# A shorter first chunk of the contraction, and x transposed by a product with a diagonal matrix

## The chip, the core and the metric

One NeuronCore of one Trainium2 chip runs the kernel. Its engines work side by side, each on its own instructions in program order: PE (matrix products and transposes; PEld is its weight load), DVE and ACT (elementwise work), POOL, and SP, which here issues nearly all DMA. The metric is the device time of one execution in microseconds (us), lower is better.

## What is computed

A transformer block over 256 tokens of width 2048. The input is normalised per token, scaled and shifted by vectors that come from a second input c through the large matrix ada_w, and projected by w_in; two attention branches, an output projection and a feed-forward part follow.

```python
c_act = jax.nn.silu(c)
mod = c_act @ ada_w[l] + ada_b[l]
sh1, sc1, gt1, sh2, sc2, gt2 = jnp.split(mod, 6, axis=-1)
h = rms_norm(x, norm1_g[l]) * (1.0 + sc1[:, None]) + sh1[:, None]
proj = h @ w_in[l]
...
x = x + gt1[:, None] * ((g_gla * y_gla + g_moba * y_moba) @ w_out[l])
h = rms_norm(x, norm2_g[l]) * (1.0 + sc2[:, None]) + sh2[:, None]
a, u = jnp.split(h @ w_ffn_in[l], 2, axis=-1)
x = x + gt2[:, None] * ((jax.nn.silu(a) * u) @ w_ffn_out[l])
```

All weights are float32. Each product is made of three float32r products: a weight tile and an h tile are each split into a high part and the rest (low part), and high x high, high x low and low x high are summed.

## The kernel before

**Tiling.** The contraction of the input projection has 2048 rows of w_in, 16 K tiles of 128. Its columns are cut into twenty blocks of 512, of which 0 to 15 take part in the stages below: in blocks 2, 3 and 8 to 15 tokens stand on partitions (`prod_tok`, six products of 128x512 for one K tile), in 0, 1 and 4 to 7 columns do (`prod_T`, twelve of 128x256). One K tile of one block is called a unit below.

**Chunks and stages.** h needs G = norm1_g (1 + scale) and SH = shift, which are columns of silu(c) @ ada_w. They are computed in chunks of K tiles, CHUNKS. While stage i of `plan` runs products with the K tiles whose h is known, the next chunk of ada_w streams in and is summed up in the background. `plan` lists by stage the blocks and up to which K tile each goes: the first stage takes ten blocks to K tile 2, the second takes those ten and blocks 0 to 5 to K tile 4, then ten to 8, and six to 12. A block's partial sum is left in PSUM, and moved by ACT (L356) where it is the block's first, or added by DVE (L358, L360) to what it had.

**ada_w.** The first chunk is multiplied on PE (L155, `on_pe`), then summed over partitions by L180. The other chunks are summed on DVE: the first step is L163, the fifteen further ones L161, each over [128, 1024] (512 where the chunk has two K tiles). Behind the sixteenth, PE sums over partitions (L186), ACT copies the result (`rowsum`, L189), PE transposes it (L192), DVE makes G and SH (L199 to L201), and `make_h` makes h of the chunk's K tiles: its high part on ACT (L298), a copy (L299), its low part on DVE (L300). The background generator is advanced after each weight tile by `pace`.

**Weights.** `w_tiles`: SP issues a load of a raw tile (two K tiles by 512 columns; rawp, ten buffers, shared with x and ada_w), ACT makes the high part (L126), DVE the low part (L127), into five buffers each. Two blocks' accumulators are open at a time (four PSUM tiles).

**The head.** Four loads bring x. ACT squares it in eight pieces of 512 with sums (L264), DVE adds them up (L265), ACT takes the root (L258), DVE multiplies all of x by it in eight pieces (L269). `x_T` transposes two K tiles by four transposes on PE (L278) and copies them (L281), all eight of these pairs before the first product. Behind the first stage come late loads on SP (`wglr`, `gn`, four of `w2`), which the gated attention needs.

**What sets the order.** A scheduler lays the instructions of each engine out in a fixed row when the kernel is built, with offsets that pull some ahead: weight parts (HP), h (HPH), evictions (HPE). On the chip each engine goes through its row in order.

Of the kernel before, what the change touches and what calls it, by code (L numbers as in the profile page):

```python
# [8 lines left out]
F32 = mybir.dt.float32  # L9
# [16 lines left out]
CHUNKS = (2, 2, 4, 4, 4)  # L26
# [14 lines left out]
def block_kernel(ctx, tc, x, c, ada_w, ada_b, norm1_g, w_in, gate_w2, gate_b, gla_norm_g,  # L41
# [31 lines left out]
    xv = x.rearrange("(m p) (j n) -> m p j n", p=P, n=W)  # L73
    xs = [[None] * 4 for _ in range(2)]
    for j in (0, 2):
        for m in range(2):
            t = rawp.tile([P, 2, W], F32, name="x", tag="raw")
            nc.sync.dma_start(t, xv[m, :, j:j + 2, :])
            xs[m][j], xs[m][j + 1] = t[:, 0], t[:, 1]

# [23 lines left out]
    cs = const.tile([P, KT], F32, name="cs")  # L104
    act(cs, cT, AF.Silu)

# [9 lines left out]
    def w_tiles(w_ap, k0, k1, c0, ncols=W):  # L116
        """tiles of the contraction by ncols columns: (first K tile, [(hi, lo), ...])"""
# [22 lines left out]
    def gemv(src, width, acc, on_pe, start=False):  # L140
        """src: [p, k, 2, width] columns of ada_w. acc: sums over partitions to (what it held, with start) +
        silu(c) @ those columns; with on_pe, to the columns of group i over partitions 64*i..64*i+63 of its first half"""
# [28 lines left out]
    def ada_scale_shift(which, k0, n, on_pe):  # L171
        """G = norm_g * (1 + scale), SH = shift, for columns of tiles k0..k0+n, column on partition"""
# [5 lines left out]
        if on_pe:  # L178
# [3 lines left out]
        else:  # L182
            # the sum over partitions of quarter g to partitions 32g.., then columns of it to partitions
# [19 lines left out]
    def ada_gate(idx, dst):  # L203
        """dst[j] = columns j of the gate, the same on each partition"""
# [48 lines left out]
    ss = const.tile([P, 2, 4], F32, name="ss")  # L253
    rstd = const.tile([P, 2], F32, name="rstd")
    junk = const.tile([P, W], BF16, name="junk")

# [5 lines left out]
    for j in range(4):  # L262
        for m in range(2):
            act(junk, xs[m][j], AF.Square, accum_out=ss[:, m, j:j + 1])  # L264
    nc.vector.tensor_reduce(rstd, ss, AX.X, ALU.add)  # L265
    row_rstd(rstd, rstd, D)
    for j in range(4):
        for m in range(2):
            ts(xs[m][j], xs[m][j], rstd[:, m:m + 1], None, ALU.mult)  # L269
# [3 lines left out]
    def x_T(kp):  # L273
        ps = ax_ps()
        for i in range(2):
            k = 2 * kp + i
            for m in range(2):
                nc.tensor.transpose(ps[:, i * T + m * P:i * T + (m + 1) * P],  # L278
                                    xs[m][k // 4][:, (k % 4) * P:(k % 4 + 1) * P], ident)
        xnT[kp] = slot("xnT")  # L280
        (nc.vector.tensor_copy if kp % 2 else nc.scalar.copy)(xnT[kp], ps)  # L281

    first = ada_scale_shift(0, 0, kn, True)
    for i in range(8):
        if i == 7:
            w_first = w_tiles(w_in, 0, 2, GG)
            w_got = [next(w_first)]
        next(first)
        x_T(i)
# [13 lines left out]
    def prod_tok(ps, m, hi, lo, wt, k0, first, last):  # L303
        """ps[token, col] += sum over the given tiles of h^T w, for token tile m"""
# [8 lines left out]
    def prod_T(ps, i, hi, lo, wt, k0, first, last):  # L313
        """ps[col, (two col tiles, token)] += sum over the given tiles, for column tiles 2i, 2i+1; one group"""
# [27 lines left out]
    def in_block(bi, k0, k1):  # L342
        """adds tiles k0..k1 of the contraction to block bi"""
        kind, c0, scale, func = blocks[bi]
        ps = [mm_ps(), mm_ps()]
        for k, g in w_got or w_tiles(w_in, k0, k1, c0):
            for i in range(2):
                (prod_T if kind == "T" else prod_tok)(ps[i], i, hTh, hTl, g, k, k == k0, k + 2 == k1)
# [24 lines left out]
    def build_masks():  # L373
# [7 lines left out]
        # keep s xor t where t > s, else 999  # L381
# [7 lines left out]
        for i in (0, 2):  # L389
            # keep 0 where t - s >= 0  # L390
# [3 lines left out]
    def gla_gate(k):  # L394
        """adds tile k to the gate's low rank product, one of four partial sums"""
# [417 lines left out]
```

## Time and profile before

| | us |
|---|---|
| median of three runs | 1471.33 (1468.92 to 1472.06) |
| profiled execution, span | 1469.6 |
| PE busy | 1441.1 (98%) |
| DVE busy | 1034.8 (70%) |
| ACT busy | 694.7 (47%) |
| granted PE clock, mean | 0.997 |
| DMA over the span | 249 GB/s |

The span is from the first to the last instruction. A matmul's busy time overlaps the next one's, so spacing is read from the chain of waits, which gives start to start. By the trace the first product of the projection starts at 26.85 us, the second stage at 58.34, the third at 125.30; the four stages are over by about 255, and the rest of the span, over 1200 us, is the other parts.

### The profile page before, as it was taken

Reading aid. Unit: us, or ns where it says so; the run is one execution under the profiler, and the core shown is the slowest. Engines: PE = TensorE matmul, PEld = TensorE weight load, DVE = VectorE, ACT = ScalarE, POOL = GpSimd, SP = SyncE. Lnnn points to the kernel's source line nnn. Section 1 sums busy time; section 2 is a strip of 40 time slices with the busy share of each in tenths; the row PEclk is TensorE's granted clock in tenths of the full one; section 3 lists DMA queues with packets and bytes.
Section 4 is the critical chain, followed back from the end, with each engine's and each line's share of the span. In section 5 each row is a group of like instructions: output and inputs, shape, how many; then the busy total and the mean of one; then the engine's idle time right before and its main releaser. Section 6 shows DMA issues by size and latency. Waiting matters only on the chain.

```text
span 1469.6 us, 19460 instructions
## 1 busy us (share of the span) xinstructions
PE 1441.1 (98%) x7304; PEld 1202.0 (82%) x7304; DVE 1034.8 (70%) x1196; ACT 694.7 (47%) x921; POOL 11.1 (1%) x28
## 2 busy tenths in 40 slices
PE   6999999999999999999999999999999999999997
PEld 3787899998788878888888778888888888888887
DVE  4798988997799989797696677544555445554554
ACT  5645344635557544444654444444343444444443
POOL 1000000000000000000000000000000000000000
PEclk9999999999999999999999999999999999999999
DMA  9999999895546999999588888655666666666641
GB/s 332 328 315 344 340 317 328 255 358 174 180 151 202 367 332 336 332 312 362 176 304 267 271 264 296 188 184 187 196 192 196 190 188 189 192 189 209 198 153 58
DMA packets 191934, 365.61 MB, mean 249 GB/s; under 512 B 13880, under 2 KB 31516, under 8 KB 191840
## 3 DMA queue, kind: packets, MB, share of 16 engines
q1 hardware_dynamic: 189792, 361.15, 74.9%
q10 hardware_dynamic: 2048, 3.22, 0.7%
q8 instruction: 57, 0.93, 0.2%
q14 instruction: 37, 0.30, 0.1%
HBM read 362.23 MB, written 2.10 MB: 248 GB/s over the span
## 4 chain that ended last, share of the span: by engine, by line
PE 91%; DMA 5%; DVE 3%; issue 1%; ACT 1%; ACTq 0%; DVEq 0%
PE mm L311 25%; PE mm L309 25%; PE mm L310 25%; DMA araw<-in_ada_w_dram 4%; PE mm L325 3%; PE mm L323 3%; PE mm L324 3%; DVE wlo L127 1%; PE ax L619 1%; PE ax L444 1%; DVE acc L161 1%; DMA x<-in_x_dram 1%; PE ax L397 0%; ACT whi L126 0%; PE ax L278 0%
## 5 line engine op out<-in xcount | busy, mean ns | idle before, releaser
L127 DVE TENSOR_TENSOR wlo<-raw,whi 128x1024 fp32r<-128x1024 f32 x488 | 595.1, 1223 | 338.8 <-ACT whi L126 331.6
L126 ACT CAST whi<-raw 128x1024 fp32r<-128x1024 f32 x488 | 512.6, 1053 | 660.6 <-PE mm L311 478.7
L309 PE MATMUL mm<-whi,h2h 128*128 128x512 f32 x704 | 274.5, 390 | 1.3 <-ACT h2h L699 1.3
L310 PE MATMUL mm<-wlo,h2h 128*128 128x512 f32 x704 | 274.9, 391 | 0.1
L311 PE MATMUL mm<-whi,h2l 128*128 128x512 f32 x704 | 274.8, 391 | 0.0
L161 DVE SCALAR_TENSOR_TENSOR acc<-araw,cs,acc 128x1024 f32<-128x1024 f32 (+1 forms) x184 | 227.6, 1237 | 27.2 <-DMA araw<-in_ada_w_dram 26.1
L311 PE MATMUL mm<-whi,tl 128*128 128x512 f32 (+1 forms) x552 | 200.7, 364 | 0.0
L309 PE MATMUL mm<-whi,th 128*128 128x512 f32 (+1 forms) x552 | 200.4, 363 | 0.0
L310 PE MATMUL mm<-wlo,th 128*128 128x512 f32 (+1 forms) x552 | 200.2, 363 | 0.0
L309 PE MATMUL mm<-whi,hTh 128*128 128x512 f32 x448 | 176.7, 398 | 3.0 <-ACT hTh L298 3.0
L310 PE MATMUL mm<-wlo,hTh 128*128 128x512 f32 x448 | 176.4, 394 | 0.6 <-DVE wlo L127 0.6
L311 PE MATMUL mm<-whi,hTl 128*128 128x512 f32 x448 | 176.7, 395 | 0.0
L309 PEld LDWEIGHTS mm<-whi,h2h 128*128 128x128 f32 x704 | 132.2, 188 | 29.2 <-ACT h2h L699 2.2
L310 PEld LDWEIGHTS mm<-wlo,h2h 128*128 128x128 f32 x704 | 132.2, 188 | 27.8 <-DVE wlo L127 0.5
L311 PEld LDWEIGHTS mm<-whi,h2l 128*128 128x128 f32 x704 | 132.2, 188 | 26.9 <-DVE h2l L700 0.2
L310 PEld LDWEIGHTS mm<-wlo,th 128*128 128x128 f32 x552 | 104.2, 189 | 16.3 <-issue 0.4
L311 PEld LDWEIGHTS mm<-whi,tl 128*128 128x128 f32 x552 | 104.3, 189 | 15.9 <-issue 0.4
L309 PEld LDWEIGHTS mm<-whi,th 128*128 128x128 f32 x552 | 104.3, 189 | 15.6
L324 PE MATMUL mm<-hTl,whi 128*128 128x256 f32 x384 | 108.8, 284 | 0.0
L323 PE MATMUL mm<-hTh,whi 128*128 128x256 f32 x384 | 108.6, 284 | 0.0
L325 PE MATMUL mm<-hTh,wlo 128*128 128x256 f32 x384 | 108.1, 284 | 0.0
L309 PEld LDWEIGHTS mm<-whi,hTh 128*128 128x128 f32 x448 | 84.5, 189 | 21.5 <-ACT hTh L298 3.7
(201 smaller groups left out, 1283.0 us busy)
## 6 DMA issues: line engine op xcount, KB each, us to landing
araw<-in_ada_w_dram SPq DMA_DIRECT2D x176, 512.0 KB, 5.6
raw<-in_w_ffn_in_dram SPq DMA_DIRECT2D x176, 512.0 KB, 3.7
raw<-in_w_in_dram SPq DMA_DIRECT2D x160, 512.0 KB, 5.6
raw<-in_w_ffn_out_dram SPq DMA_DIRECT2D x88, 512.0 KB, 4.6
raw<-in_w_out_dram SPq DMA_DIRECT2D x32, 512.0 KB, 7.4
araw<-in_ada_w_dram SPq DMA_DIRECT2D x32, 256.0 KB, 6.0
raw<-in_w_up_moba_dram SPq DMA_DIRECT2D x16, 512.0 KB, 5.1
raw<-in_w_up_gla_dram SPq DMA_DIRECT2D x16, 512.0 KB, 7.8
```

Of the source, the lines that this page charges most:

```text
L126: nc.scalar.copy(hi, raw)
L127: tt(lo, raw, hi.bitcast(F32), ALU.subtract)
L161: stt(a, vq, cs[:, k:k + 1], a, ALU.mult, ALU.add)
L309: mm(ps, lhsT=xh, rhs=wh, start=f, stop=False)
L310: mm(ps, lhsT=xh, rhs=wl, start=False, stop=False)
L311: mm(ps, lhsT=xl, rhs=wh, start=False, stop=l)
L323: mm(o, lhsT=wh[:, sl], rhs=xh, start=f, stop=False)
L324: mm(o, lhsT=wh[:, sl], rhs=xl, start=False, stop=False)
L325: mm(o, lhsT=wl[:, sl], rhs=xh, start=False, stop=l)
L444: mm(ps[:, s], lhsT=e[:, s], rhs=e[:, s], start=True, stop=True)
L619: nc.tensor.transpose(ps[:, q * T + m * P:q * T + (m + 1) * P], src[m][:, (2 * i + q) * P:(2 * i + q + 1) * P], ident)
```

## The change

The chunks become 1, 1, 2, 4, 4, 4, and `plan` gets one stage more: ten blocks to K tile 1, blocks 0 to 5 to K tile 2, then the ten and the six to K tile 4 (three and two units of each), the last two as before. In a stage whose blocks take an odd number of K tiles the last weight tile is half as wide.

x is squared in four pieces of 1024, two on ACT and two on DVE; a dummy root ahead of them loads ACT's table early. x itself is left as it is: DVE multiplies the unit matrix by the norm factor of each token half (`diag`), and `x_T` multiplies x by that in full float32 products where it had transposes. Only the first pair of K tiles is done ahead of the first product; the other seven are written behind blocks 15, 10, 11, 6, 7, 8 and 9 of the first stage; in PE's row the scheduler has put seven of their 28 products between the sum over partitions of the first chunk and the first product, and 21 between the products of the first stage. A chunk of one K tile that is summed on DVE takes its partition sum as columns straight away.

```diff
-CHUNKS = (2, 2, 4, 4, 4)
+CHUNKS = (1, 1, 2, 4, 4, 4)
...
+    act(cs0, epst, AF.Sqrt)
...
-        if on_pe:
+        if n == 1 and not on_pe:
+            for i in range(2):
+                mm(ps[:, 2 * i:2 * i + 2], lhsT=acc[:, i * P:(i + 1) * P], rhs=ones[:, 0:2], start=True, stop=True)
+            pv = ps[:, 0:4].rearrange("p (e i a) -> p e a i", e=2, a=2)[:, :, 0:1]
+        elif on_pe:
...
-    for j in range(4):
-        for m in range(2):
-            act(junk, xs[m][j], AF.Square, accum_out=ss[:, m, j:j + 1])
+    for i, (m, j, t) in enumerate(xw):
+        sq = slots.tile([P, 2 * W], BF16, name="sq", tag="slot")
+        if i % 2:
+            nc.vector.tensor_tensor_reduce(sq, t, t, 1.0, 0.0, ALU.mult, ALU.add, ss[:, m, j:j + 1])
+        else:
+            act(sq, t, AF.Square, accum_out=ss[:, m, j:j + 1])
...
-    for j in range(4):
-        for m in range(2):
-            ts(xs[m][j], xs[m][j], rstd[:, m:m + 1], None, ALU.mult)
+    for m in range(2):
+        ts(diag[:, m], ident, rstd[:, m:m + 1], None, ALU.mult)
...
-                nc.tensor.transpose(ps[:, i * T + m * P:i * T + (m + 1) * P],
-                                    xs[m][k // 4][:, (k % 4) * P:(k % 4 + 1) * P], ident)
+                mm(ps[:, i * T + m * P:i * T + (m + 1) * P], lhsT=xs[m][k // 4][:, (k % 4) * P:(k % 4 + 1) * P],
+                   rhs=diag[:, m], start=True, stop=True)
...
-    for i in range(8):
-        if i == 7:
-            w_first = w_tiles(w_in, 0, 2, GG)
+    for i in range(4):
+        if i == 3:
+            w_first = w_tiles(w_in, 0, kn, GG)
             w_got = [next(w_first)]
         next(first)
-        x_T(i)
+    x_T(0)
...
-    plan = [[(b, 2) for b in (12, 13, 14, 15, 10, 11, 6, 7, 8, 9)],
+    plan = [[(b, 1) for b in (12, 13, 14, 15, 10, 11, 6, 7, 8, 9)],
+            [(b, 2) for b in range(6)],
...
+            if st == 0 and bi not in (12, 13, 14):
+                x_T(next(later_x))
```

Three places show how the rows of the engines move. The first is DVE at the end of the stage behind which h of K tiles 4 to 7 is made. In the kernel before, `acc_674` is the sum of the chunk, `acc_1340` that of the next chunk, `wlo` are low parts of weights:

```order
L161 SCALAR_TENSOR_TENSOR acc_674<-araw_1167,cs_108,acc_674 128x1024
L127 TENSOR_TENSOR wlo_1172<-raw_1170,whi_1171 128x1024
L161 SCALAR_TENSOR_TENSOR acc_674<-araw_1200,cs_108,acc_674 128x1024
L127 TENSOR_TENSOR wlo_1211<-raw_1209,whi_1210 128x1024
L127 TENSOR_TENSOR wlo_1254<-raw_1252,whi_1253 128x1024
L127 TENSOR_TENSOR wlo_1306<-raw_1304,whi_1305 128x1024
L127 TENSOR_TENSOR wlo_1324<-raw_1322,whi_1323 128x1024
L163 TENSOR_SCALAR acc_1340<-araw_1341,cs_108 128x1024
L199 TENSOR_TENSOR G0_124<-ax_1246,scb_114 128x4
```

In the changed kernel, at the same place, `acc_819` is the sum of the chunk and `acc_1459` that of the next; `r4` and `r5` are evictions of blocks 4 and 5 (L372 is L360 of before, L131 L127, L165 and L167 are L161 and L163, L207 is L199):

```order
L372 SCALAR_TENSOR_TENSOR r4_1_740<-mm_1325,r4_1_740 128x512
L131 TENSOR_TENSOR wlo_1469<-raw_1467,whi_1468 128x1024
L372 SCALAR_TENSOR_TENSOR r5_0_775<-mm_1371,r5_0_775 128x512
L372 SCALAR_TENSOR_TENSOR r5_1_776<-mm_1372,r5_1_776 128x512
L165 SCALAR_TENSOR_TENSOR acc_819<-araw_1235,cs_108,acc_819 128x1024
L131 TENSOR_TENSOR wlo_1490<-raw_1488,whi_1489 128x1024
L165 SCALAR_TENSOR_TENSOR acc_819<-araw_1272,cs_108,acc_819 128x1024
L131 TENSOR_TENSOR wlo_1515<-raw_1513,whi_1514 128x1024
L165 SCALAR_TENSOR_TENSOR acc_819<-araw_1319,cs_108,acc_819 128x1024
L167 TENSOR_SCALAR acc_1459<-araw_1460,cs_108 128x1024
L165 SCALAR_TENSOR_TENSOR acc_1459<-araw_1485,cs_108,acc_1459 128x1024
L165 SCALAR_TENSOR_TENSOR acc_1459<-araw_1506,cs_108,acc_1459 128x1024
```

The evictions of block 5, the last block of the stage, have come to DVE, and three steps of the chunk's sum now stand behind them; G follows behind the last row shown.

The second place is PE there. In the changed kernel (L337 is L325 of before, L194 and L200 are L186 and L192, L321 and L322 are L309 and L310), `mm_1372` is the second accumulator of block 5 and `hTh_222` holds h of K tiles 4 and 5:

```order
L336 MATMUL mm_1372<-hTl_229,whi_1374 128x256
L337 MATMUL mm_1372<-hTh_221,wlo_1375 128x256
L194 MATMUL ax_1356<-acc_819,ones_89 32x256 x4
L200 MATMUL ax_1363<-ident_84,rowsum_1361 128x128 x2
L321 MATMUL mm_1421<-whi_1424,hTh_222 128x512
L322 MATMUL mm_1421<-wlo_1425,hTh_222 128x512
```

In the kernel before, the sum over partitions stood some thirty products ahead of the end of block 5; it now stands behind the last one.

The third place is SP at the end of the first stage, in the changed kernel; `raw_536` is the first weight load of the second stage:

```order
L128 DMA raw_469<-in_w_in_dram 128x512
L128 DMA raw_500<-in_w_in_dram 128x512
L583 DMA wglr_104<-in_w_in_dram 128x16x16
L583 DMA gn_105<-in_gla_norm_g_dram 128x256
L583 DMA w2_103<-in_gla_gate_w2_dram 16x512 x4
L128 DMA raw_536<-in_w_in_dram 128x2x512
L153 DMA araw_567<-in_ada_w_dram 128x2x256 x2
```

The late loads stand behind the loads of the first stage and ahead of those of the second, as before, but behind ten tiles of half the size.

## Rows read from the trace of the kernel before

**Rows 1.** The page: busy time by engine, and the chain that ended last.

```profile
PE 1441.1 (98%) x7304; PEld 1202.0 (82%) x7304; DVE 1034.8 (70%) x1196; ACT 694.7 (47%) x921; POOL 11.1 (1%) x28
...
PE 91%; DMA 5%; DVE 3%; issue 1%; ACT 1%; ACTq 0%; DVEq 0%
```

**Rows 2.** Timeline of the head: start, duration, engine, line, operation.

```profile
13.55 1.28 ACT L258 ACT_TABLE_LOAD   x1 [0.27 <-DVE rstd L265]
...
15.38 3.26 DVE L269 TENSOR_SCALAR x<-x,rstd 128x512 f32<-128x512 f32 x8
...
23.55 1.06 PE L155 MATMUL ax<-araw,cpad 128*32 128x256 f32 x12
...
26.20 1.09 ACT L298 ACTIVATE hTh<-xnT,SH,G 128x256 fp32r<-128x256 f32 x2 [1.17 <-DVE G L200]
...
26.85 0.61 PE L309 MATMUL mm<-whi,hTh 128*128 128x512 f32 x1 [1.14 <-ACT hTh L298]
```

**Rows 3.** Busy time of each engine by window, granted clock, DMA share, GB/s.

```profile
0.00:10.00 10.00, 0.40 (x1) 0.18 (x1) 0.18 (x1) 5.59 (x11) 3.92 (x19) 1.00 0.80 254
10.00:20.00 10.00, 8.75 (x60) 3.98 (x61) 5.21 (x16) 5.91 (x14) 0.00 (x0) 1.00 1.08 353
...
26.80:31.00 4.20, 4.15 (x11) 3.19 (x12) 3.61 (x6) 2.93 (x5) 0.00 (x0) 0.59 1.07 370
...
58.00:67.00 9.00, 8.66 (x35) 6.12 (x36) 7.60 (x11) 5.75 (x8) 0.00 (x0) 1.00 1.05 390
67.00:100.00 33.00, 33.00 (x212) 29.84 (x211) 32.34 (x36) 12.29 (x14) 0.00 (x0) 1.00 0.90 307
...
125.30:184.00 58.70, 58.70 (x307) 48.27 (x308) 53.58 (x61) 24.59 (x30) 1.54 (x1) 1.00 0.94 330
```

**Rows 4.** Pieces of the chain of waits: start, time, engine, line.

```profile
18.45 0.59 PE ax L278 x4
...
28.31 0.43 PE mm L310
...
58.34 0.74 PE mm L309 x2
...
63.78 0.23 PE mm L309
...
123.77 0.12 PE mm L323
...
405.40 1.78 PE ax L444 x16
```

**Rows 5.** DVE groups up to 300 us: count, then busy and mean ns.

```profile
L127 DVE TENSOR_TENSOR wlo<-raw,whi 128x1024 fp32r<-128x1024 f32 x93 | 112.4, 1220 | 10.4 <-ACT whi L126 9.9
L161 DVE SCALAR_TENSOR_TENSOR acc<-araw,cs,acc 128x1024 f32<-128x1024 f32 x59 | 75.4, 1278 | 0.2
L358 DVE TENSOR_TENSOR r<-mm,r 128x512 f32<-128x512 f32 x52 | 34.9, 686 | 8.7 <-PE mm L311 7.9 <-PE mm L325 0.6
...
L163 DVE TENSOR_SCALAR acc<-araw,cs 128x1024 f32<-128x1024 f32 x3 | 2.2, 748 | 0.0
```

**Rows 6.** Timeline of SP: the late loads and the weight load behind them.

```profile
41.18 0.37 SPq L567 DMA_DIRECT2D wglr<-in_w_in_dram  x1
41.88 6.15 SPq L567 DMA_DIRECT2D gn<-in_gla_norm_g_dram  x1
...
50.01 0.91 SPq L124 DMA_DIRECT2D raw<-in_w_in_dram  x2
```

**Rows 7.** Timeline at the end of the second stage, as in rows 2.

```profile
120.17 0.64 PE L186 MATMUL ax<-acc,ones 128*32 128x256 f32 x8
...
122.09 0.16 DVE L200 TENSOR_TENSOR G<-G,vT 128x4 f32<-128x4 f32 x1
...
123.85 0.28 PE L325 MATMUL mm<-hTh,wlo 128*128 128x256 f32 x1
...
125.30 0.50 PE L309 MATMUL mm<-whi,hTh 128*128 128x512 f32 x1 [1.17 <-ACT hTh L298]
```

More of the change, by code (lines that the diff above doesn't have):

```diff
@@ L74, in block_kernel @@
     xs = [[None] * 4 for _ in range(2)]
+    xw = []
     for j in (0, 2):
@@ L79, in block_kernel @@
             xs[m][j], xs[m][j + 1] = t[:, 0], t[:, 1]
+            xw.append((m, j // 2, t.rearrange("p a n -> p (a n)")))
     ident = const.tile([P, P], F32, name="ident")
@@ L104, in block_kernel @@
     cs = const.tile([P, KT], F32, name="cs")
+    cs0 = const.tile([P, 1], F32, name="cs0")
     act(cs, cT, AF.Silu)
+    act(cs0, epst, AF.Sqrt)
     vps = ax_ps()
@@ L250, in kx @@
         return t if m is None else t[:, m * P:(m + 1) * P]
-    ss = const.tile([P, 2, 4], F32, name="ss")
+    ss = const.tile([P, 2, 2], F32, name="ss")
     rstd = const.tile([P, 2], F32, name="rstd")
     junk = const.tile([P, W], BF16, name="junk")
+    diag = const.tile([P, 2, P], F32, name="diag")
     def row_rstd(dst, ssum, n):
@@ L347, in in_block @@
             for i in range(2):
-                (prod_T if kind == "T" else prod_tok)(ps[i], i, hTh, hTl, g, k, k == k0, k + 2 == k1)
+                (prod_T if kind == "T" else prod_tok)(ps[i], i, hTh, hTl, g, k, k == k0, k + len(g) == k1)
             background(pace[0])
@@ L552, in block_kernel @@
     done = {}
+    later_x = iter(range(1, 8))
     for k in range(kn):
         make_h(k)
-    for st in range(4):
+    for st in range(5):
         nk = CHUNKS[st + 1]
         bg.append(ada_scale_shift(0, kn, nk, False))
-        nt = sum((k1 - done.get(b, 0)) // 2 for b, k1 in plan[st])
+        nt = sum((k1 - done.get(b, 0) + 1) // 2 for b, k1 in plan[st])
         pace[0] = (KT * nk // 4 + 0.5) / (nt - 2)
```

## The prediction

> **What bounds the kernel now.** I read the page first: PE is busy for 98% of the span and its products are 91% of the chain that ended last [rows 1]. So a step is worth something only where PE waits, or where PE gets other work to do. Next come the head's timeline [rows 2], to see what the first product waits for, and the windows by stage [rows 3], to see what stands beside PE: DVE is full in 67–100 (32.34 of 33 us), but only 53.58 of 58.70 us in 125.3–184. Then the end of the second stage [rows 7]: the last product of its block 5 begins at 123.85, and PE waits only 1.17 us for the next h. From 125.30 on PE is busy without a gap to 184, and nothing in the program behind that point is changed. So the whole forecast is one question: **when does the first product that uses K tile 4 start, 125.30 before?** Everything behind it moves along with it.
>
> **The head.** In 0–10 us DMA moved 254 GB/s, 2.5 MB, of which x is 2.1 [rows 3]: x has landed by about 10. Before, the squares, a table load (13.55, 1.28 us) and eight scalings (15.38, 3.26 us) come ahead of the transposes, and the first product starts at 26.85 [rows 2]. Now half of the squares goes to DVE, the table load goes ahead, and the scalings go away. Two 1024-wide squares on DVE are not in this trace; the 1024-wide operations of rows 5 take 1.22 to 1.28 us, so rstd stands near 13.5 and the first K tile pair, transposed and copied, near 15.5. Then the chunk's load decides: 2.1 MB instead of 4.2. In 512-byte pieces I estimate 300 GB/s, since 1 KB pieces gave 353 (10–20) and mostly 2 KB ones 390 (58–67) [rows 3]: 7 us, so 17; at 353 it is 5.9, so 16. From the last partial product (23.55 for 1.06 us) to the first product it took 2.24 us [rows 2]; a last batch of 0.6 in front of that makes **19.8**. The order puts seven later products of x between, which can hide in the wait for G or cost 1.6 us more. Bounds 18.8 and 21.8, so the gain in the head is 5.0 to 8.0 us.
>
> **Given back in the first stage.** Ten units (one K tile of one block) instead of twenty. A unit with tokens on partitions is six products of 0.23 us, one with columns there twelve of 0.12 [rows 4]: 8 x 1.36 + 2 x 1.44 = 13.8 us. The first products run at half clock, since the granted clock of 26.8–31 is 0.59 [rows 3]: eight of 0.43 instead of 0.23 [rows 4], some 1.8 us with the first, in both kernels. Now 21 products of x with the diagonal stand between the units, on the path. The nearest row is L444, f32 128x128 products: 16 records in 1.78 us, two records to each product (112 for 56 in the code), 0.22 us each [rows 4]: **4.7 us**, with 1 us for changing between kinds. A transpose of rows 4 takes 0.59/4 = 0.15 us, so each product costs 0.07 us more than the transpose it replaces. Of this price the Trainium skill, "TensorE: Matmul & The Clock Gate" (Terms), says that transpose mode is four times faster for FP32, which speaks against the products; four times 0.15 would be 0.6 us, so 12.6 us for the 21 and 7.9 more in the sum. The L444 row, a plain f32 product, doesn't bear that out.
> Their copies go to ACT and DVE by turns and lie beside products. So the first stage ends at 19.8 + 13.8 + 1.8 + 4.7 + 1.0 = 41.1; before, with twice the units, the second stage begins at 58.34 [rows 4].
>
> **The second stage is short of data.** It has six blocks of two units, 4 x 2 x 1.44 + 2 x 2 x 1.36 = 17.0 us of PE, but loads 3.1 MB of weights and 4.2 MB of ada_w: at 390 GB/s 18.8 us. And ahead of its loads on SP's queue, by the order, are the late loads: before, the issue of gn took 6.15 us and the next weight's issue came at 50.01, 8.8 us after the first of them [rows 6]. Before that was hidden by first-stage products until 58. Now it comes when PE has nothing left; at least 5.5 us shows. Change of h between the stages costs about 1.8 us more (cast, low part and h, one behind the other). 41.1 + 1.8 + 17.0 + 6 = **66** for the start of the third stage; 60.5 if most of the hole hides, 70 if the weights come later still.
>
> **The third stage.** PE: ten blocks of three units and six of two, 24 x 1.36 + 6 x 1.44 + 8 x 1.44 + 4 x 1.36 = 58.3 us. DVE: 16 low parts of 1.14 from start to start (1.22 in rows 5), 10 half ones of 0.62, 16 operations of the sum at 1.19, 20 evictions of 0.60, and **12 evictions that ACT did before** (blocks 0 to 5 now add to what the second stage left): 62.6 us, some of it ahead of the stage or behind block 5. So both engines are full, and block 5 ends at E = 66 + 58.3 + 1 = **125.3**; before, 124.1 [rows 7]. The lead of the head has gone by then: the x products, the change between the stages and the hole in the loads have taken it.
>
> **The bubble behind it, the main term.** The order of DVE before puts the last step of the sum (L161) four low parts ahead of the stage's end. Now the two evictions of block 5, which wait for its last product, stand ahead of three of the sixteen steps, and each step alternates with a low part. PE's next instruction behind block 5 is the sum over partitions (L194), which needs the sixteenth. So after E, DVE does: r5_1 0.9 with its wait, step 1.19, low part 1.14, step 1.19, low part 1.14, step 1.28 [rows 5], to E + 6.9. L194, the rowsum copy, the transposes and G took 2.08 us before (120.17 to the end of G at 122.25 [rows 7]), to E + 9.0. But G stands on DVE behind a first step of 0.7 us and two further ones of the next chunk, to E + 9.9. G and SH 0.4, h 0.6 and the start: **E + 11.05**, where it was E + 1.2. Nothing covers it: PE is in order, and every product behind needs this h. After such an idle time the clock may fall as it was low at 26.8–31 [rows 3]: 1.8 us again if so, nothing if not; the 1.17 us gap at 124 shows no drop (125.3–184 has 1.00). I take 1.8, as an idle time of eleven us is nearer to the start, where PE had also had little to do. The Trainium skill, "TensorE: Matmul & The Clock Gate" (Part 1), says that an idle engine falls to 1.2 GHz and that sustained work brings 2.4 back; by it the 1.8 stands, without it the time is 1.8 less.
> Sum: 125.3 + 11.05 + 1.8 = 138.15 against 125.30: +12.85. The profiled execution's span is 1469.6, the median of the runs 1471.33, so 1.7 lies around it or is spread between runs; 1469.6 + 12.85 + 1.7 = 1484.2, rounded **1484**.
>
> **Rivals.**
> *Lead kept to the third stage.* The hole in DMA hides behind the x products: the stage starts at 60.5, E = 119.8, the next at 119.8 + 12.85 = 132.7: +7.4, **1478.7**. For it: x's buffers come free through the first stage. Against: gn's 6.15 us.
> *The lead pays for the bubble.* First product at 18.8, no hole, no stall between the stages: 18.8 + 13.8 + 1.8 + 4.7 + 17.0 = 56.1, E = 114.4 if DVE keeps up, plus 11.05: 125.45, no clock loss: **1471.5**. It becomes a gain only when E is under 111.4, which no sum here reaches, unless the operations on DVE's queue in the bubble also go quicker. It ends not slower than before.
> *Starved longer.* 512-byte pieces go slower than 300 GB/s, or a product of x takes 0.42 us and not 0.22 (21 times 0.2 is 4.2), and the third stage starts at 70: E = 129.3, **1488**. For it: nothing in this trace moves 512-byte pieces in bulk. Against: 64 partial products kept up with 1 KB ones.
> *The first product isn't earlier.* The change doesn't do what it says: the products with the diagonal run at half clock in the head (0.45 us), the DVE squares wait on the last x tile, and T0 stays at 25 or later; then the rest adds to it, **1489** or more.
>
> **How the numbers follow.** Forecast 0.60, lead kept 0.18, starved 0.12, lead pays 0.06, first product not earlier 0.04. The range from 1476 to 1489 takes in both ends of the second stage and of the clock, and leaves out some 0.15. A difference of 0.2%, 2.9 us, is about what a measurement of this kernel can tell from no change. Faster by more: 0.03; within: 0.05; slower: 0.92.
>
> **What the profile after would show.** Right: first product near 20; DMA under 200 GB/s for some us around 40–50 with PE idle beside; the third stage starting at 60–70; then, behind block 5's last product near 125, PE idle for some 10 us while DVE alternates sum steps and low parts, and a granted clock of 0.5 after it. From there on the same spacing as before. Wrong: block 5 ending before 112, or the gap behind it under 5 us, which would mean that the sum was through when block 5 ended.

## The result, and the profile after

The changed kernel took 1494.94 us (median of four runs, 1493.02 to 1497.99) against 1470.63 for the kernel before: 24 us slower, ratio 1.0163 with a 95% interval of 1.015 to 1.0175. The forecast was 1484 with a range of 1476 to 1489, so the sign was right and the size was not: the time lies above the range. The profiled execution has a span of 1491.2 us, 21.6 more than before.

The first rows to read are PE's waits up to 300 us: engine and line, what was waited for, total, times, longest.

```profile
PE ax L194 <- DVE acc L165: 7.6, 1, 7.6
PE mm L335 <- ACT hTh L310: 3.2, 1, 3.2
PE mm L337 <- DVE wlo L131: 2.2, 3, 1.4
PE mm L321 <- ACT hTh L310: 1.9, 1, 1.9
```

Before, the longest wait of PE behind its first product was 1.17 us [rows 7]. Now there are two places with longer ones at a stage's end: one near 130 (the first and the last row), where PE waits for the sum over ada_w and then for h, and one that the second row shows, which the prediction did not have. The third row lies in the second stage, where waits for the two parts of the weights add up to 5.4 us. The timeline of the first place, behind block 5's last product:

```profile
129.03 0.28 PE L337 MATMUL mm<-hTh,wlo 128*128 128x256 f32 x1
129.73 1.28 DVE L372 SCALAR_TENSOR_TENSOR r<-mm,r 128x512 f32<-128x512 f32 x2
...
130.93 1.27 DVE L165 SCALAR_TENSOR_TENSOR acc<-araw,cs,acc 128x1024 f32<-128x1024 f32 x1
132.12 1.22 DVE L131 TENSOR_TENSOR wlo<-raw,whi 128x1024 fp32r<-128x1024 f32 x1
...
133.26 1.28 DVE L165 SCALAR_TENSOR_TENSOR acc<-araw,cs,acc 128x1024 f32<-128x1024 f32 x1
...
134.45 1.22 DVE L131 TENSOR_TENSOR wlo<-raw,whi 128x1024 fp32r<-128x1024 f32 x1
...
135.59 1.28 DVE L165 SCALAR_TENSOR_TENSOR acc<-araw,cs,acc 128x1024 f32<-128x1024 f32 x1
...
136.92 1.08 PE L194 MATMUL ax<-acc,ones 128*32 128x256 f32 x8 [7.61 <-DVE acc L165]
...
140.09 0.15 DVE L207 TENSOR_TENSOR G<-ax,scb 128x4 f32<-128x4 f32 x1
...
141.13 0.80 PE L321 MATMUL mm<-whi,hTh 128*128 128x512 f32 x1 [1.95 <-ACT hTh L310]
```

This is the row of instructions that the prediction read: two evictions, then step, low part, step, low part, step. From 129.31 to 141.13 PE has nothing but the sum over partitions and its transposes, 1.77 us. The second place, 144 us further on:

```profile
272.96 0.28 PE L337 MATMUL mm<-hTh,wlo 128*128 128x256 f32 x1
273.16 1.04 ACT L130 CAST whi<-raw 128x1024 fp32r<-128x1024 f32 x1 [2.53 <-PE mm L336]
...
274.24 1.23 DVE L131 TENSOR_TENSOR wlo<-raw,whi 128x1024 fp32r<-128x1024 f32 x1 [0.27 <-ACT whi L130]
275.38 0.15 DVE L207 TENSOR_TENSOR G<-ax,scb 128x4 f32<-128x4 f32 x1
...
276.42 0.73 PE L335 MATMUL mm<-hTh,whi 128*128 128x256 f32 x4 [3.18 <-ACT hTh L310]
```

PE had the sum's transposes done at 271.2, but on DVE G stands behind a low part whose high part waits for a weight buffer, which the stage's last products free. So G waits for the products that it should have run beside. The granted clock is 0.50 at 277.9 to 281.3, so the place costs more than its wait.

To see where time goes I line the two traces up by work: each 128x512 product counts 0.227 us and each 128x256 one 0.12 (their spacing, [rows 4]), and the table gives the time at which a kernel has done that many us of products of h and weights, as a difference to the kernel before, whose own times stand in the second line. It is worked out from one trace of each kernel; the runs differ by a us or two. All kernels of the experiments are in it.

```
work us           1     10     25     60     85     95    160    220    400   1200
before         28.5   38.6   54.0   92.9  118.9  133.8  202.0  267.6  490.4 1320.4
after          -5.9   -4.0   +7.4   +6.0   +6.2  +17.4  +18.1  +23.1  +21.9  +21.5
g_first        -6.9   -5.0   +6.6   +5.2   +5.4  +17.5  +16.1  +13.9  +14.2  +15.7
sum_first      -6.5   -4.4   +7.8   +6.3  +15.5  +11.6  +11.6   +9.4   +9.3  +13.7
evict_act      -6.7   -4.3   +6.9   +5.5   +6.4   +3.0   +1.6   -0.5   -0.9   +4.4
late_later     -6.6   -4.4   +2.7   +5.5   +5.5  +18.7  +19.4  +24.9  +24.8  +25.4
late_only      -6.8   -4.5   +2.9   +0.4   +0.7  +12.1  +12.9  +13.7  +13.8  +14.1
late_g         -6.1   -4.0   +3.8   +1.3   +1.6  +12.4  +11.0   +8.8   +8.4   +9.4
late_last      -6.4   -4.9   +2.2   -0.7   +2.7   +1.5   +0.1   -2.0   -3.1   -0.4
late_evict     -6.3   -4.4   +3.3   +0.3   +1.3   -2.1   -0.1   -2.1   -2.1   +0.4
x_only         -0.6   -0.2   +1.5   +2.9   +2.4   +2.4   +2.4   +2.2   +1.8   +1.5
chunks_only    +0.2   +0.8   +9.7   +8.2   +8.4  +20.3  +21.0  +26.4  +26.8  +26.4
x_head         +2.4   +2.7   +9.9   +8.5   +8.7  +20.9  +21.6  +27.2  +26.9  +27.9
x_transpose    -4.1   -2.9   +6.9   +5.4   +5.7  +16.8  +17.6  +22.6  +21.7  +19.9
pool_lo        -6.7   -4.9   +6.7   +6.5  +11.2   +7.8   +6.8   +4.7   +4.5   +8.5
late_pool      -4.5   -3.1   +3.8   +2.5   +9.0   +5.9   +8.4   +6.4   +6.1   +9.1
before_g       -0.3   -0.5   +0.3   +0.5   +1.4   +0.5   -1.0   -3.0   -3.4   -2.6
```

The row of the changed kernel: 5.9 us ahead at the first products; by the end of the second stage, near 31 us of work, the lead is gone and 5 to 7 us behind stand in its place; level through the third; 11 us lost at its end and on the clock behind it; 5 at the second place; 1.6 won back later (behind 300 us PE's waits add up to 3.8 us, before to 5.0). The lead was in good part work put off and not work saved: between the first stage's products stand 21 products of x, 4.4 us from start to start, that the kernel before had done as transposes ahead of its first product. When the second stage begins, at 42.98, the kernel before has passed the same amount of work 0.7 us earlier. The windows of the changed kernel name what stood beside it (columns as in [rows 3]):

```profile
10.00:20.00 10.00, 7.88 (x75) 4.24 (x75) 4.37 (x13) 2.82 (x7) 0.00 (x0) 1.00 0.90 259
22.00:30.00 8.00, 7.87 (x38) 6.07 (x37) 6.02 (x12) 6.22 (x13) 0.00 (x0) 1.00 0.95 283
36.00:40.00 4.00, 4.00 (x29) 3.69 (x28) 2.25 (x6) 3.65 (x7) 0.00 (x0) 1.00 0.53 131
48.00:60.00 12.00, 8.45 (x42) 6.26 (x42) 11.20 (x15) 4.28 (x7) 0.00 (x0) 1.00 1.08 366
68.00:129.50 61.50, 60.62 (x342) 51.58 (x340) 59.12 (x71) 27.00 (x33) 0.00 (x0) 1.00 0.96 332
129.50:141.00 11.50, 1.77 (x10) 0.49 (x10) 11.43 (x15) 1.95 (x4) 0.00 (x0) 0.72 0.83 276
141.00:145.00 4.00, 3.87 (x11) 2.08 (x12) 3.96 (x6) 3.51 (x8) 0.00 (x0) 0.53 1.05 393
```

DMA falls to 131 GB/s at 36 to 40, behind the late loads; then it runs full (366) while PE has 8.45 of 12 us to do. In the third stage DVE is nearly as full as PE. The late loads on SP, and the weight load behind them:

```profile
31.59 2.98 SPq L583 DMA_DIRECT2D gn<-in_gla_norm_g_dram  x1
34.63 2.57 SPq L583 DMA_DIRECT2D w<-in_gla_gate_w_dram  x4
37.30 0.40 SPq L128 DMA_DIRECT2D raw<-in_w_in_dram  x1
```

### The profile page after: what moved, and what is told of

Its sections match the earlier page's. It is cut to its first block, busy times and chain, and to the rows that moved or that the text cites. A ratio compares the mean times of both kernels' runs of the same rounds, so it can differ in the third digit from the quotient of the medians.

```text
span 1491.2 us, 19618 instructions
## 1 busy us (share of the span) xinstructions
PE 1447.1 (97%) x7338; PEld 1207.7 (81%) x7338; DVE 1051.0 (70%) x1235; ACT 692.5 (46%) x920; POOL 9.6 (1%) x28
## 4 chain that ended last, share of the span: by engine, by line
PE 86%; DMA 6%; DVE 6%; issue 1%; ACT 1%; SPq 1%; ACTq 0%; DVEq 0%
PE mm L321 24%; PE mm L322 24%; PE mm L323 24%; DMA araw<-in_ada_w_dram 4%; PE mm L337 3%; PE mm L336 3%; PE mm L335 3%; DVE wlo L131 2%; DVE acc L165 2%; PE ax L635 1%; DVE r L370 1%; PE ax L456 1%; DMA raw<-in_w_in_dram 1%; DMA x<-in_x_dram 1%; PE ax L409 1%
## 5 line engine op out<-in xcount | busy, mean ns | idle before, releaser
L131 DVE TENSOR_TENSOR wlo<-raw,whi 128x1024 fp32r<-128x1024 f32 (+1 forms) x498 | 596.8, 1201 | 357.1 <-ACT whi L130 352.6
L130 ACT CAST whi<-raw 128x1024 fp32r<-128x1024 f32 (+1 forms) x498 | 515.2, 1036 | 693.0 <-PE mm L323 485.0
L321 PE MATMUL mm<-whi,h2h 128*128 128x512 f32 x704 | 274.6, 390 | 1.3 <-ACT h2h L715 1.3
L322 PE MATMUL mm<-wlo,h2h 128*128 128x512 f32 x704 | 275.0, 391 | 0.1
L165 DVE SCALAR_TENSOR_TENSOR acc<-araw,cs,acc 128x1024 f32<-128x1024 f32 (+2 forms) x199 | 234.8, 1180 | 31.8 <-DMA araw<-in_ada_w_dram 30.4
L321 PE MATMUL mm<-whi,th 128*128 128x512 f32 (+1 forms) x552 | 200.3, 363 | 0.0
L322 PE MATMUL mm<-wlo,th 128*128 128x512 f32 (+1 forms) x552 | 200.2, 363 | 0.0
L321 PE MATMUL mm<-whi,hTh 128*128 128x512 f32 x448 | 177.4, 399 | 3.0 <-ACT hTh L310 1.9
L322 PE MATMUL mm<-wlo,hTh 128*128 128x512 f32 x448 | 177.1, 395 | 1.9 <-DVE wlo L131 1.9
L321 PEld LDWEIGHTS mm<-whi,h2h 128*128 128x128 f32 x704 | 132.2, 188 | 29.0 <-ACT h2h L715 2.2
L322 PEld LDWEIGHTS mm<-wlo,h2h 128*128 128x128 f32 x704 | 132.2, 188 | 27.7 <-DVE wlo L131 0.5
L322 PEld LDWEIGHTS mm<-wlo,th 128*128 128x128 f32 x552 | 104.2, 189 | 16.3 <-issue 0.4
L321 PEld LDWEIGHTS mm<-whi,th 128*128 128x128 f32 x552 | 104.4, 189 | 15.5
L337 PE MATMUL mm<-hTh,wlo 128*128 128x256 f32 x384 | 108.9, 286 | 2.2 <-DVE wlo L131 2.2
L321 PEld LDWEIGHTS mm<-whi,hTh 128*128 128x128 f32 x448 | 84.3, 189 | 22.9 <-ACT hTh L310 2.3
```

The lines of the kernel that those rows point to most:

```text
L130: nc.scalar.copy(hi, raw)
L131: tt(lo, raw, hi.bitcast(F32), ALU.subtract)
L165: stt(a, vq, cs[:, k:k + 1], a, ALU.mult, ALU.add)
L321: mm(ps, lhsT=xh, rhs=wh, start=f, stop=False)
L322: mm(ps, lhsT=xh, rhs=wl, start=False, stop=False)
L337: mm(o, lhsT=wl[:, sl], rhs=xh, start=False, stop=l)
```

## The experiments

Times are medians; each is set beside the kernel before on the same chip, by the ratio with its interval.

**The order of G, alone** (`g_first`): the sum over partitions, its copy, the transposes, G and SH get a higher priority.

```diff
+        with tc.high_priority(offset=HPH if which == 0 and not on_pe else 0):
             ps = ax_ps()
...
             tt(g, pv[:, 1], cols(scb[:, which], k0), ALU.add)
```

> The changed kernel, in which the instructions from the sum over partitions to G and SH get a higher priority in the row, for the four chunks of norm1 that are summed on DVE. Nothing else is changed. In the trace of the changed kernel PE stood idle for 12 us at 129 to 141 and for 3.5 us at 273; before the second, G stood on DVE behind a low part that waited for the stage's last product. Theory A (the order on DVE's row makes both gaps): the second gap goes, as G now stands some twenty rows earlier there, and 4 to 5 us of the difference with it; the first stays at 11 to 12 us, since the three steps of the sum still stand behind the evictions of block 5. About 1490. Theory B (DVE has too much to do, whatever the order): G earlier only moves the wait to a low part, the gap at 273 goes but comes back within the next stage; 1494 to 1495.

1487.03 us, 1.0107 (1.0092 to 1.0122): 8 us less than the changed kernel, and more than the 4 to 5 of theory A. The table shows +17.5 at 95, as in the changed kernel (+17.4), but 13.9 at 220 where that had 23.1. The second gap is gone, as theory A had it, and the trace is 2 us better at the end of the fourth stage (16.1 against 18.1 at 160) and 2 more at the second place; the same order won as much there in the kernel before (`before_g`).

**The steps of the sum ahead of the evictions** (`sum_first`).

```diff
+                with tc.high_priority(offset=prio):
...
+        yield from gemv(src, n * P, acc, on_pe, prio=(200 if (k0, n) == (4, 4) else 0) if which == 0 else 0)
```

> As g_first, and the sixteen steps of the sum for K tiles 4 to 7 get a higher priority, so that the sixteenth and G stand ahead of block 5's evictions on DVE. Theory A (order): the 12 us gap falls to 1 to 3 us, the low clock behind it goes, block 5 ends 0 to 3 us later; 11 to 14 us less than the changed kernel with the second gap closed too: 1476 to 1481. Theory B (load): DVE was full from 80 to 140 in the changed kernel, so the steps that go ahead push back the weights' low parts; block 5 ends as much later as the gap shrinks, but for the 5.7 us of low parts for the next stage that DVE had done by then: 1485 to 1490.

1483.21, 1.0081 (1.0066 to 1.0096): 4 us less than `g_first`, where theory A's 1476 to 1481 would have been 6 to 11; the time lies between the two theories. The timeline, of DVE and then of PE, shows where the rest went:

```profile
122.43 1.27 DVE L166 SCALAR_TENSOR_TENSOR acc<-araw,cs,acc 128x1024 f32<-128x1024 f32 x1
123.62 3.48 DVE L131 TENSOR_TENSOR wlo<-raw,whi 128x1024 fp32r<-128x1024 f32 x3
127.03 1.87 DVE L372 TENSOR_TENSOR r<-mm,r 128x512 f32<-128x512 f32 x3
```

```profile
127.85 0.76 PE L323 MATMUL mm<-whi,hTh 128*128 128x512 f32 x1 [4.01 <-DVE r L372]
```

The wait for the sum has become a wait for an accumulator that DVE has not yet emptied: the evictions now come late, behind a step and three low parts. The granted clock behind this wait is 0.50 (127.8 to 132). DVE is full from 80 to 128, so its load may be the second part of the loss (theory B); the order of its row at this place is a rival.

**The two halves of the change** (`x_only`: chunks and plan of before with the new x; `chunks_only`: the new chunks and plan with x as before). From the diff of `x_only` against the changed kernel:

```diff
-CHUNKS = (1, 1, 2, 4, 4, 4)
+CHUNKS = (2, 2, 4, 4, 4)
...
-    plan = [[(b, 1) for b in (12, 13, 14, 15, 10, 11, 6, 7, 8, 9)],
-            [(b, 2) for b in range(6)],
+    plan = [[(b, 2) for b in (12, 13, 14, 15, 10, 11, 6, 7, 8, 9)],
```

> The kernel before with the x part alone: squares split between ACT and DVE, table loaded early, diagonal products, one pair of K tiles ahead of the first product and seven between blocks of the first stage; chunks and plan as before. Theory A: no gap at the stage's end, since the order there is as before; the first product comes 2 to 3 us earlier (no scalings, fewer x products ahead of it, the same 4.2 MB of ada_w), and 24 products of 0.22 us less the transposes saved come into the first stage: between -1 and +4 us, 1470 to 1475. Rival (the x products between blocks are what costs): +6 or more, over 1477.

> The kernel before with the chunks and the plan alone: x squared on ACT, scaled on DVE and transposed in the head as before. Theory A (the new stage and its order make the loss): both gaps as in the changed kernel, first product at 22 to 24, no x products in the first stage: within 3 us of the changed kernel, 1491 to 1497. Rival (x products): 1480 or less.

`x_only` took 1474.42, 1.0027 (1.0015 to 1.0039), `chunks_only` 1497.39, 1.0173 (1.0158 to 1.0189). The chunks and the plan make the loss. Neither half starts the products earlier by more than 0.6 us (first column): the smaller chunk needs the shorter way of x, and the shorter way of x needs the smaller chunk. Together they bring 5.9 there.

**x products: price and place** (`x_transpose`, `x_head`).

```diff
-                mm(ps[:, i * T + m * P:i * T + (m + 1) * P], lhsT=xs[m][k // 4][:, (k % 4) * P:(k % 4 + 1) * P],
-                   rhs=diag[:, m], start=True, stop=True)
+                nc.tensor.transpose(ps[:, i * T + m * P:i * T + (m + 1) * P],
+                                    xs[m][k // 4][:, (k % 4) * P:(k % 4 + 1) * P], ident)
```

```diff
-    x_T(0)
+    for i in range(8):
+        x_T(i)
...
-            if st == 0 and bi not in (12, 13, 14):
-                x_T(next(later_x))
```

> The changed kernel with transposes in place of the 32 products of x with the diagonal, at the same places; x is not scaled, so the norm factor is left out of the result. What a product costs more than a transpose: by the kernel before, 0.22 against 0.11 to 0.15 us. If the second stage waits for data anyway, the 2 to 3 us are lost again by its end: within 1 us of the changed kernel, 1494 to 1496. If the time goes through to the end: 1492 to 1493. A product that costs four times a transpose would give 1488 or less.

> The changed kernel with all eight pairs of x products ahead of the first product, as the transposes were in the kernel before. First product 3 to 5 us later, at 24 to 26; the first stage shorter by 21 times 0.22 = 4.7 us; x's buffers are free before the first stage begins, so that the loads of the second stage can be issued earlier. If it was the x products and their buffers in the first stage that held the second stage back: 3 us or more under the changed kernel. If the second stage is held by its own volume and DVE: within 2 us of 1495.

`x_transpose` took 1496.34, 1.0166 (1.0138 to 1.0194): no difference. Its trace doesn't show the price alone: its granted clock was 0.51 at 18 to 25, where the changed kernel's was 1.00, and its first product came 1.0 us later (22.55 against 21.59). At 25 us of work, where both wait for data, it is 0.5 ahead (+6.9 against +7.4). `x_head` took 1502.01, 1.0196 (1.0167 to 1.0226), 5 to 7 us over the changed kernel. Its products begin 8 us later, not the 3 to 5 expected, and 2.5 of these are still there behind the second stage. So the place of the x products matters a little; whether their price matters is not shown.

**The late loads** (`late_later` behind the second stage, `late_last` behind the third on top of `sum_first`, `late_only` behind the third on the changed kernel, `late_g` the same on `g_first`). The diff of `late_only`; `late_later` has 1 and 0 for the numbers:

```diff
-        if st == 0:
+        if st == 2:
             for dst, src in late_loads:
                 nc.sync.dma_start(dst, src)
...
             make_h(k)
-            gla_gate(k)
+            if st > 1:
+                gla_gate(k)
```

> The changed kernel, in which the late loads (wglr, gn, w2), and the gate's products with them, stand behind the second stage and no longer behind the first. In the trace of the changed kernel the second stage, 17 us of products, ran from 43 to 67, and work that was 4 us ahead at 35 us was 7 us behind at 61. The prediction put 5.5 us or more of that on the late loads. Theory A (they make the hole): the second stage ends 4 to 6 us earlier, and the end of the run comes 3 to 5 us earlier, 1490 to 1492, less what the loads cost at their new place. Rival (the stage is short of data by its volume, 7.3 MB for 17 us of products, wherever the late loads stand): the second stage ends within 1.5 us of 67, and the run within 2 us of 1495.

1496.36, 1.0158 (1.0135 to 1.0181): no gain. At 25 us of work it is 4.7 us earlier (+2.7), and the third stage begins 4.0 us earlier (63.96), but by 60 us of work that is lost again: the loads' hole comes where DVE and the third stage's loads should have run. Its window shows it:

```profile
56.00:64.00 8.00, 7.62 (x63) 6.34 (x62) 3.08 (x6) 5.33 (x9) 0.00 (x0) 1.00 0.76 209
```

> sum_first, with the late loads and the gate's products behind the third stage instead of the first. With the loads behind the second stage the hole only changed its place: the second stage ended 4.5 us earlier, but DVE then had nothing to do for 3.6 us at 60 to 64, and block 5 ended where it did. Behind the third stage DMA has 10 to 17% left. If the third stage is bound by DVE from its first low part to its last (theory B), starting it 4 to 5 us earlier brings its end 4 to 5 us earlier: 1478 to 1480. If the order of the rows or PE's own work sets the end, nothing comes through: 1482 to 1485.

1472.91, 1.0010 (0.9999 to 1.0021), 10 us under `sum_first` where 3 to 5 were expected. 5.6 of it is there at 25 and 7 at 60; the rest appears behind it (2.7 against 15.5 at 85). The same two rows of the waits of PE, of `sum_first` and then of `late_last`:

```profile
PE mm L323 <- DVE r L372: 4.0, 1, 4.0
PE mm L323 <- DVE r L374: 0.7, 1, 0.7
```

```profile
PE mm L323 <- DVE r L372: 1.7, 1, 1.7
PE mm L323 <- DVE r L374: 0.7, 1, 0.7
```

The wait is 2.3 us shorter, and the reason is again a row that moved without being touched. In `sum_first` DVE's step is followed by three low parts and then by the evictions; here by one:

```profile
115.37 1.27 DVE L166 SCALAR_TENSOR_TENSOR acc<-araw,cs,acc 128x1024 f32<-128x1024 f32 x1
116.56 1.21 DVE L131 TENSOR_TENSOR wlo<-raw,whi 128x1024 fp32r<-128x1024 f32 x1
117.70 2.47 DVE L372 TENSOR_TENSOR r<-mm,r 128x512 f32<-128x512 f32 x4
```

Two low parts of 1.14 are the 2.3 us. So of the 10 us some belong to the scheduler's row and not to the data; no run keeps the row and moves the loads alone.

> The changed kernel with the late loads and the gate's products behind the third stage, and nothing else: no priorities. The step of the sum behind block 5's evictions stays. If the late loads alone are what starves the second and the third stage, block 5 ends 6 to 8 us earlier than in the changed kernel and the 12 us gap behind it stays: 1486 to 1489. If the time comes through only together with the earlier sum (DVE idles at the stage's end either way), within 3 us of 1495. If most of the 10 us that late_last gained over sum_first came from an accident of the rows, 1484 or less.

> late_only with the instructions from the sum over partitions to G at a higher priority, as in g_first. By the single steps: 8 us less than late_only, since G stands ahead of low parts in the later stages, while the gap behind the third stage stays at 10 to 12 us: 1478 to 1481. late_last, which differs in the steps of the sum alone, took 1472.9; the difference is what their place behind block 5's evictions costs.

`late_only` took 1485.67, 1.0099 (1.0084 to 1.0114); `late_g` 1481.51, 1.0070 (1.0053 to 1.0087). In `late_only` DMA gives 370 GB/s at 36 to 40, where the changed kernel had 131. Block 5 ends at 123.8, 5.5 us earlier than in the changed kernel, and the gap behind it stays at 11.9 us, by much the same rows of DVE:

```profile
124.12 0.68 DVE L372 SCALAR_TENSOR_TENSOR r<-mm,r 128x512 f32<-128x512 f32 x1
...
130.18 1.08 PE L194 MATMUL ax<-acc,ones 128*32 128x256 f32 x8 [6.40 <-DVE acc L165]
...
135.68 0.80 PE L321 MATMUL mm<-whi,hTh 128*128 128x512 f32 x1 [2.24 <-ACT hTh L310]
```

In `late_only` the second gap has gone by itself (13.7 at 220): G stands earlier in DVE's row there, at 266.3, while the stage's products still run. That is 4 of its 9 us, and on `g_first`, where this gap was closed already, moving the loads is worth 5.5 (`late_g`). And `late_last` against `late_g`, which differ in the priority of the steps alone: 8.6 us. The prediction put 11.65 on this place (11.05 less 1.2, and 1.8 for the clock). Without the late loads the order is worth most of that; with them it is worth 4, and how much of the difference is the row of `sum_first` at its wait stays open.

**DVE's load** (`evict_act` on `sum_first`, `late_evict` on `late_last`; `pool_lo` and `late_pool` on the same two).

```diff
-                if k0 == 0:
+                if k0 == 0 or (bi < 6 and k0 == 2):
                     act(res[bi][i], ps[i], AF.Copy if k1 < KT or func is None else func, scale=scale)
```

```diff
-                tt(lo, raw, hi.bitcast(F32), ALU.subtract)
+                (nc.gpsimd.tensor_tensor if on_pool else tt)(lo, raw, hi.bitcast(F32), ALU.subtract)
```

> sum_first, with the twelve evictions of blocks 0 to 5 at the end of the third stage on ACT, as they are in the kernel before; they only copy, so the products of these blocks with K tiles 0 and 1 are left out of the result. In sum_first G stands ahead of block 5's evictions, but PE still waits 4.4 us at 123 and DVE is full from 80 to 130. Theory B (what is left there is DVE's load): 12 times 0.6 us leave DVE, the wait at 123 and the low clock behind go, 4 to 6 us less than sum_first: 1477 to 1479. Theory A (order alone): within 1.5 us of sum_first, 1482 to 1485.

1475.08, 1.0018 (1.0007 to 1.0030): 8 us under `sum_first`. The 4 us wait of PE and the loss behind it are gone (+3.0 at 95 against +11.6). Theory B, and more than its 4 to 6 us. That the evictions no longer stand in DVE's row also takes them out from behind the three low parts, so the run shows that they cost this time on DVE, by load and place together.

> late_last with the twelve evictions of blocks 0 to 5 at the end of the third stage on ACT as copies (the products of these blocks with K tiles 0 and 1 are left out of the result). late_last was 0.7 us ahead of the kernel before at 60 us of product work and 2.7 behind at 85. If that is DVE's load alone, the lead stays and with the earlier G 2 to 4 us less than late_last come out: 1468 to 1471. If it is the order of the low parts or the loads, no change: 1472 to 1474.

1472.74, 1.0006 (0.9992 to 1.0020): no difference from `late_last`. The expected 2 to 4 us did not come. The trace has 3.6 us of them at 95, and they are gone at 160; the runs do not show them at all. So the evictions on DVE cost the whole run nothing once the loads have moved; what took the 3.6 us in the fourth stage is not shown.

> sum_first, with five of the sixteen full low parts of the third stage on POOL, which is idle there. Five times 1.14 = 5.7 us leave DVE; nothing else is changed, and the result is complete. Theory B (DVE's load is what is left of the gap): 4 to 6 us less than sum_first, 1477 to 1479, as where the evictions were moved. Against it: POOL may take longer for a low part than the five weight buffers can bridge, or slow DVE while it runs; then 1482 or more.

> pool_lo and late_last together. If both say what theory B says, the third stage starts 4 to 5 us earlier and needs 5.7 us less of DVE: 1473 to 1476. If only one of the two acts, as the single runs show.

`pool_lo` took 1480.57, 1.0058 (1.0042 to 1.0074), 2.6 us under `sum_first`; `late_pool` 1480.79, 1.0056 (1.0039 to 1.0074), 8 over `late_last`. POOL's low parts are slow, and DVE's became slower beside them (groups of `pool_lo`, POOL in 60 to 140, DVE in 80 to 140):

```profile
L137 POOL TENSOR_TENSOR wlo<-raw,whi 128x1024 fp32r<-128x1024 f32 x5 | 13.9, 2781 | 101.5 <-ACT whi L136 101.5
```

```profile
L137 DVE TENSOR_TENSOR wlo<-raw,whi 128x1024 fp32r<-128x1024 f32 x13 | 17.8, 1383 | 0.0
...
L137 DVE TENSOR_TENSOR wlo<-raw,whi 128x512 fp32r<-128x512 f32 x7 | 8.5, 1208 | 0.0
```

**G earlier in the kernel before** (`before_g`, the diff of `g_first`).

> The kernel before, with the instructions from the sum over partitions to G and SH at a higher priority, for the chunks of norm1 that are summed on DVE. In its trace PE waits 1.4 us for h at 124 and 1.0 us at 57. If the order there is what costs them, 1 to 2.5 us less than the kernel before: 1469 to 1470.5; if they are the length of the chain from the sum to h, no difference, 1471 to 1472.

1468.90, 0.9981 (0.9970 to 0.9992): 2.7 us less than the kernel before, and the only version whose interval lies below 1. It did not come where I looked for it: the waits at 57 and 124 stay (+0.5 at 95). It came behind the last two stages' ends, 1.5 us by 160 us of work and 2 more by 220.

## Why the prediction was wrong, point by point

**The head** held, near the late bound: first product at 21.59, bounds 18.8 to 21.8, taken 19.8. The term that was off is the load: DMA gave 259 GB/s at 10 to 20, most of it in 512-byte pieces, where I had estimated 300, and the last partial products began at 18.94 and not at 17.

**The first stage** held in its sum, and that is luck in part. Its last product of x ended at 41.8, forecast 41.1. The products did not start at half clock (1.00 in 22 to 30), so 1.8 us did not come, and the start 1.8 us later took their place. The x products cost what was taken: the 21 between the units 4.4 us from start to start, 0.21 each, against 4.7.

**The second stage** was short of data, as said: the third began at 68.0, forecast 66 with 60.5 to 70. That the late loads make a hole is shown: without them there the third stage begins 4.0 us earlier in `late_later`, 4.5 in `late_only`, 5.5 in `late_last` against `sum_first` and 2.8 in `late_g` against `g_first`. The sign that I named for it was not right: the low stretch of DMA, at 36 to 40, lay beside products that still ran (PE 4.00 of 4), and PE's idle time came behind it, with DMA full. And the hole is not all: without the late loads the stage still takes 22.2 us for 17.0 us of products (`late_last`, 40.61 to 62.83).

**The third stage** took 61.3 us to block 5's end, forecast 59.3. DVE was busy for 59.12 of 61.5 us. So E was 129.3 and not 125.3. This is the value of the rival "starved longer", but by chance: there the stage began at 70 and took 59.3 us, here it began at 68.0 and took 2.0 longer.

**The gap behind it** was there with the row of instructions that I read in the order: 11.8 us against 11.05. L194 came 7.6 behind E (forecast 6.9), G 10.8 (9.9). So the main term was right in mechanism and near in size. The clock behind it was 0.53 in 141 to 145, and cost 1.5 us by the two traces (15.82 behind at the first product, 17.36 at 95), where 1.8 were taken. The Trainium skill, "TensorE: Matmul & The Clock Gate" (Part 1), says that an idle engine falls to the lower level; the row agrees: PE, with 1.77 us of work in 11.8, came back near the lower of the two levels.

**The step that failed** is the sentence that behind 125.30 nothing is changed and everything moves along. The code there is unchanged, but its rows are not: at the end of the fifth stage the scheduler put G behind a low part that waits for the stage's last products, and 5.0 us were lost there, 0.7 at another stage's end. `g_first` moves G and the gap is gone. The prediction rests on the order at one stage end out of four. With E 4.0 later, the gap 0.8 longer, the clock 0.3 cheaper, 5.7 lost behind and 1.6 won back, the 12.85 of the forecast become 21.5 in the trace; the runs' median lies 2 us over the profiled execution. The second term that was too small is E, by 2.0 us in the second stage and 2.0 in the third; alone it would have given some 1488, as in the rival, inside the range, and the step behind 125.30 took the time out of it.

**What else the prediction had wrong** is that it took the costs as a sum. The runs show that they depend on each other: the same change of order is worth 4 us or 8.6, moving the late loads behind the second stage nothing (`late_later`), behind the third 5.5 (`late_g`), 9 (`late_only`) or 10 (`late_last`), moving the evictions 8 or nothing. Part of this is that each edit also moved rows that it did not name. The stage waits for whichever of data, DVE's load and DVE's order is last, and a step taken from one is given to the next.

**Left open:** `late_last` is level with the kernel before and not ahead, though it keeps the earlier start, 6.4 us at the first products. The first stage takes 4.7 of these, 4.2 of them for the x products that were put off: its second stage begins 1.7 us ahead at the same work. The rest goes in the second stage (+2.2 at 25, and 0.3 ahead when the third begins), where PE has 10 of 12 us to do at 48 to 60 beside 377 GB/s. That it is the volume of that stage, 7.3 MB for 17 us of products, fits those rows, but no run made the volume smaller.

## What to carry to other kernels

Before costing an edit that adds a stage or a tile size, compare the fixed order of the engines at **every** stage end, also where the source is untouched, and look for an instruction that feeds the next stage and stands behind one that waits for this stage's last product. Where two kernels have the same work in another sequence, line their traces up by work done and read where the difference steps. A gain at the start is worth only what the next stages' data and side engines can follow, and work that was only put off has to be taken from it: of the 5.9 us here, 4.4 were products of x that stood behind the first product instead of ahead of it.

## What the runs showed of the hardware

A subtraction of 128x1024 on POOL took, by the profile, 2.78 us on average in `pool_lo` and 3.73 us in `late_pool`, against 1.22 on DVE. Beside it DVE's own took 1.38, and the half-wide ones 1.21 where they had taken 0.69. The Trainium skill, "SBUF — State Buffer" (SBUF: two separate sides), says that the two engines share a pair of ports as an exclusive lock, also for DVE operations with two SBUF inputs; the longer rows of DVE agree with it in kind. Moving these five operations won 2.6 us in `pool_lo` and lost 8 in `late_pool`.

The granted clock was 1.00 from the first h product on in the changed kernel, where the kernel before had 0.59 [rows 3]. What PE did just ahead goes with it. In the kernel before it had waited 1.14 us, and 2.85 in `chunks_only` and 3.40 in `x_head`, whose clock was 0.66 and 0.61 in the first 4.2 us; in the changed kernel and in `x_only` products of x ran up to the first h product, and the clock stayed:

```profile
27.70:31.90 4.20, 4.20 (x13) 3.28 (x13) 4.06 (x9) 2.51 (x6) 0.00 (x0) 0.66 1.03 314
```

```profile
26.20:30.40 4.20, 4.20 (x23) 3.52 (x22) 3.59 (x6) 3.42 (x7) 0.00 (x0) 1.00 1.07 369
```

These are windows of `chunks_only` and of `x_only`. An exception is `x_transpose`: transposes ran up to its first product, but its clock had fallen at 18.0 already.
